# Latent attention's fp32 products written as three one-pass products of high and low parts

## The chip, the cores and the metric

The kernel runs on one core of a Trainium2 chip. The core has five engines, each with its own in-order queue: TensorE (PE, matrix products; its weight loads are listed as PEld), VectorE (DVE), ScalarE (ACT), GpSimd (POOL) and SyncE (SP, which issues nearly all transfers). The metric is the device time of one execution in microseconds (us): the median over runs. The profile is one further execution, with its own time.

## The reference

The reference is a decoder trunk with one layer of kind A and one of kind B, at 256 positions, width 2048. The change touches the latent attention of layer B alone:

```python
q = (rmsnorm(q_lat, g_q_lat) @ w_uq).reshape(B, S, MLA_HEADS, NOPE_DIM + ROPE_DIM)   # 12 heads, 128 + 64
q_nope = q[..., :NOPE_DIM]
q_rope = apply_rope(q[..., NOPE_DIM:], cos, sin)
# per block of 128 queries
qa = jnp.einsum('bqhn,rhn->bqhr', qn, w_uk)
s = (jnp.einsum('bqhr,bkr->bhqk', qa, c_kv) + jnp.einsum('bqhp,bkp->bhqk', qr, k_rope)) * scale
s = jnp.where(k_pos[None, :] <= q_pos[:, None], s, -jnp.inf)
p = jax.nn.softmax(s, axis=-1)
o_lat = jnp.einsum('bhqk,bkr->bqhr', p, c_kv)
return jnp.einsum('bqhr,rhv->bqhv', o_lat, w_uv)
```

All arrays are fp32. Beside it stand a four-head attention into 256 memory tokens, the output projection, a gated feed-forward network and, after both layers, a final norm.

## The kernel before

Activations lie feature-major: 128 features on the partitions, 256 positions along the free axis. Every large weight product is made of *parts*: a number is split into a high part (rounded by a copy into the type fp32r, which the TensorE multiplies in one pass) and a low part (the rest, also fp32r). Activations hold both parts side by side, high in columns 0 to 255, low in 256 to 511 (`xhl`, `qhl`, `chl`, `mainhl`). `chunk` loads a piece of a weight (`raw`), ACT copies it to `whi`, DVE subtracts to get `wlo`; `mm_fm` multiplies `whi` with all 512 columns (line 158) and `wlo` with the high 256 (line 162). `join` adds the two halves of the result (ACT copies one out of PSUM into `cr`, DVE adds). `wlo` tiles for stationary use begin 19 floats into their buffer.

The latent attention does not use parts. It runs after the projections: `values` makes the values of all heads by `gemm_tm` (lines 213 to 215) and evicts them as fp32 into `scratch`. Then a loop over six pairs of heads, `i` = 0 to 5, issues for each pair: `queries` (three 128-row blocks: two heads' plain queries and one block with both heads' rotary parts, into the fp32 tile `qn`), `keys` (two blocks into `kn`), `rotary` (one product of the rotary block with a permutation `swap`, line 857, then DVE and POOL form `qr`), `scores` per head (lines 947 to 949), `turn` (three transposes of the probabilities, line 970, copied by ACT into `pT`) and `attend` (lines 979 and 980). Scores of a pair come one iteration after its queries and keys, `turn` and `attend` one iteration later still. The memory attention (`mscores`, `mturn`, `mout`; lines 575, 599, 610) is spread over the same iterations. The last turns and attends run as hooks inside the output projection.

In `scores`, the first block of 128 queries sees 128 keys and the second 256, so each of the two products (plain and rotary) is made once with 128 columns and once with 256; between them a bf16 product with 128 columns adds the causal mask (line 948). All these products are fp32. In the hardware's records one fp32 matmul is two rows (two weight loads, two matmuls), one fp32r matmul is one row. `attend` is a 256-column and a 128-column product per head.

The program text gives priorities only. A scheduler that simulates the engines sets the order on each engine when the kernel is built; that order is then fixed, and each engine takes its instructions strictly in turn. PSUM has eight tiles, `cr` and `js` two buffers each, `raw`, `whi` and `wlo` four.

Of the kernel before, what the change touches and what calls it, by code (L numbers as in the profile page):

```python
# [8 lines left out]
F32 = mybir.dt.float32  # L9
# [60 lines left out]
class Kernel:  # L70
# [247 lines left out]
    def masks(self):  # L318
# [14 lines left out]
        self.identb = cp.tile([P, P], BF16, name="identb")  # L333
        nc.vector.tensor_copy(self.identb, self.ident)
        self.maskb = cp.tile([P, P], BF16, name="maskb")
        m = self.gp.tile([P, P], F32, name="mask")
# [257 lines left out]
    def memory_turn(self, p, pool, bufs=2):  # L594
        nc = self.nc
        acc = self.psum()
        for mb in range(2):
            for sb in range(2):
                nc.tensor.transpose(  # L599
                    acc[:, mb * S + sb * P : mb * S + (sb + 1) * P], p[:, sb, mb * P : (mb + 1) * P], self.ident  # L600
                )
        pT = self.tmp(pool, [P, 512], "pT", bufs)
        nc.scalar.activation(pT, acc, AF.Copy)
# [204 lines left out]
    def layer_b(self):  # L808
# [9 lines left out]
        with tc.tile_pool(name="lb", bufs=1) as lb:  # L818
            ctx = ExitStack()
            qhl = lb.tile([P, 4, 512], F32R, name="qhl")  # L820
            chl = lb.tile([P, 4, 512], F32R, name="chl")

            krz = lb.tile([P, 2, S], F32, name="krz")
            nc.gpsimd.memset(krz, 0.0)
            qm = lb.tile([P, MH, S], F32, name="qm1")
            lt = ctx.enter_context(tc.tile_pool(name="lt", bufs=1))

# [26 lines left out]

            def rotate(dst, a):
                acc = self.psum()
                mm(acc[:, :S], self.swap, a, start=True, stop=True)
                m = self.tmp(lb, [P, S], "rm", 1)
                nc.gpsimd.tensor_tensor(m, a, self.cosT, ALU.mult)
                tt(dst, acc[:, :S], self.sinT, ALU.mult)  # L860
                nc.gpsimd.tensor_tensor(dst, dst, m, ALU.add)
# [13 lines left out]
            def rotate_key():  # L875
# [17 lines left out]
            hl = self.ap.tile([P, NB, 512], F32R, tag="big", name=self.uid("mainhl"))  # L893
            scratch = self.ap.tile([P, NB * 512], F32, tag="xhl", name="scratch")
            v = scratch[:, : 2 * GW].rearrange("p (a c) -> p a c", a=2)
# [15 lines left out]
            scale = HD ** -0.5  # L911
            qn, qr, kn, pa, pm = {}, {}, {}, {}, {}

            def queries(pr):
                accs = [self.psum() for _ in range(3)]
                src = self.rows(wuq, pr * 2 * HD, 2 * HD)
                for c in range(0, 4, 2):
# [5 lines left out]
                    self.mm_fm(jobs, c > 0)  # L923
                qn[pr] = self.tmp(lp, [P, 3, S], "qn", 2)
                for j in (2, 0, 1):
                    self.join(accs[j], qn[pr][:, j, :])

            def keys(pr):
                kn[pr] = self.tmp(lp, [P, 2, S], "kn", 2)

                def ev(b, acc):
                    self.join(acc, kn[pr][:, b, :])

                self.gemm_fm(self.rows(wuk, pr * 256, 256), list(range(4)), 2, lambda k: chl[:, k, :], ev, nk=4)

            def rotary(pr):
                qr[pr] = self.tmp(lp, [P, S], "qr", 2)
                rotate(qr[pr], qn[pr][:, 2, :])

            def scores(h):  # L940
                pr, j = divmod(h, 2)
                sc = self.psum()
                for qb in range(2):
                    n = P * (qb + 1)
                    o = sc[:, qb * P : qb * P + n]
                    q = slice(qb * P, (qb + 1) * P)
                    mm(o, qn[pr][:, j, q], kn[pr][:, j, :n], start=True, stop=False)  # L947
                    mm(o[:, qb * P :], self.identb, self.maskb, start=False, stop=False)
                    mm(o, qr[pr][:, q], krz[:, j, :n], start=False, stop=True)  # L949
                mx = self.tmp(lp, [P, 2], "mx", 4)  # L950
# [15 lines left out]
            def turn(h):  # L966
                p = pa.pop(h)
                acc = self.psum()
                for i in range(3):
                    nc.tensor.transpose(acc[:, i * P : (i + 1) * P], p[:, i * P : (i + 1) * P], self.ident)  # L970
                pT = self.tmp(lp, [P, 512], "pT", 3)
                nc.scalar.activation(pT[:, : 3 * P], acc[:, : 3 * P], AF.Copy)
                pa[h] = pT

            def attend(h):
                pT = pa.pop(h)
                o = self.psum()
                cols = slice(h * P, (h + 1) * P)
                mm(o[:, :S], v[:, 0, cols], pT[:, :S], start=True, stop=False)  # L979
                mm(o[:, P:S], v[:, 1, cols], pT[:, S : S + P], start=False, stop=True)  # L980
                self.split(hl[:, h, :], o[:, :S])
# [4 lines left out]
            def mturn(h):  # L986
                pm[h] = self.memory_turn(pm[h], lp, 3)

# [135 lines left out]
```

## Time and profile before

| | |
|---|---|
| median of 3 runs | 2075.89 us (2075.86 to 2075.90) |
| profiled execution, its own time | 2076.27 us |
| its span | 2074.6 us |
| TensorE busy in the span | 99% |
| VectorE, ScalarE, GpSimd busy | 70%, 55%, 19% |
| TensorE clock granted | 0.998 |
| where the attention loop lies | about 1171 to 1252 us, its last two heads up to about 1270 us |

In a timeline row the columns are start (us from the span's start), duration from the first start to the last end (us), engine, line, operation, tiles written and read, shape, count and, in brackets, idle time of the engine before it with what ended it. A matmul's duration includes the time it takes to drain, which overlaps the next one; the pace of matmuls is read from the distance between starts. [...]

### The profile page before, as it was taken

The numbers are of one execution on the slowest core, as the hardware profiler recorded it, in microseconds if no ns is written. First come the engines' busy times: TensorE is split into PE (matmuls) and PEld (weight loads), VectorE is DVE, ScalarE is ACT, GpSimd is POOL, SyncE is SP. The second block draws the span as 40 slices with busy tenths as digits, with TensorE's granted clock in tenths as the row PEclk, the third lists the DMA queues.
The fourth block names the chain that finished last, engine by engine and source line by source line (L and its number), as shares of the span: only waits on it lengthen the run. The fifth ranks groups of instructions, "written<-read, shape, count | busy, mean of one in ns | idle before, by whom it ended". The sixth has DMA issues, their size and how long they took to land.

```text
span 2074.6 us, 31012 instructions
## 1 busy us (share of the span) xinstructions
PE 2064.0 (99%) x11614; PEld 1803.8 (87%) x11614; DVE 1460.5 (70%) x2150; ACT 1138.7 (55%) x1747; POOL 397.3 (19%) x387
## 2 busy tenths in 40 slices
PE   9999999999999999999999999999999999999998
PEld 8888888888888888888888888888888888888886
DVE  6655767777756877568798875777774677746875
ACT  7754654665535655455555664466653565535654
POOL 0100133322101222012254121421210222101220
PEclk9999999999999999999999999999999999999999
DMA  8575556666556666666565534566666666566664
GB/s 279 194 216 162 163 191 195 191 187 201 194 193 193 184 203 194 192 192 191 186 198 178 178 108 163 186 189 184 195 198 193 185 192 196 200 193 190 186 193 153
DMA packets 208092, 392.01 MB, mean 189 GB/s; under 512 B 14334, under 2 KB 23876, under 8 KB 207812
## 3 DMA queue, kind: packets, MB, share of 16 engines
q1 hardware_dynamic: 207364, 388.98, 60.1%
q8 instruction: 91, 1.49, 0.3%
q10 hardware_dynamic: 576, 1.05, 0.2%
q14 instruction: 61, 0.50, 0.1%
HBM read 387.88 MB, written 2.10 MB: 188 GB/s over the span
## 4 chain that ended last, share of the span: by engine, by line
PE 99%; ACT 0%; DVE 0%; issue 0%; ACTq 0%
PE ps L158 52%; PE ps L162 26%; PE ps L214 6%; PE ps L213 6%; PE ps L215 6%; PE ps L949 0%; PE ps L947 0%; PE ps L575 0%; PE ps L432 0%; PE ps L610 0%; PE ps L979 0%; PE ps L760 0%; PE ps L513 0%; PE ps L872 0%; PE ps L970 0%; PE ps L599 0%
## 5 line engine op out<-in xcount | busy, mean ns | idle before, releaser
L118 DVE TENSOR_TENSOR wlo<-raw,whi 128x1024 fp32r<-128x1024 f32 x660 | 842.8, 1287 | 453.2 <-ACT whi L117 338.6
L117 ACT ACTIVATE whi<-raw 128x1024 fp32r<-128x1024 f32 x660 | 695.6, 1058 | 677.3 <-PE ps L158 499.1
L158 PE MATMUL ps<-xhl,whi 128*128 128x512 f32 x3264 | 765.2, 390 | 0.0
L158 PEld LDWEIGHTS ps<-xhl,whi 128*128 128x128 f32 x3264 | 604.9, 188 | 121.2
L662 POOL TENSOR_TENSOR a<-js,rbc 128x256 f32<-128x256 f32 x176 | 230.7, 1323 | 1082.4 <-DVE js L264 986.7
L162 PEld LDWEIGHTS ps<-xhl,wlo 128*128 128x128 f32 x3264 | 388.9, 188 | 8.4
L162 PE MATMUL ps<-xhl,wlo 128*128 128x256 f32 x3264 | 392.2, 277 | 0.0
L158 PE MATMUL ps<-h,whi 128*128 128x512 f32 x704 | 164.8, 390 | 0.0
L665 ACT ACTIVATE c<-a,cT 128x256 f32<-128x256 f32 x176 | 105.2, 598 | 96.7 <-POOL a L662 95.2
L158 PEld LDWEIGHTS ps<-h,whi 128*128 128x128 f32 x704 | 130.4, 188 | 26.0
L214 PE MATMUL ps<-wlo,h 128*128 128x512 f32 x354 | 137.1, 388 | 0.0
L213 PE MATMUL ps<-whi,h 128*128 128x512 f32 x354 | 137.0, 388 | 0.0
L215 PE MATMUL ps<-whi,h 128*128 128x512 f32 x354 | 136.6, 388 | 0.0
L158 PE MATMUL ps<-mainhl,whi 128*128 128x512 f32 x512 | 120.1, 390 | 0.0
L158 PEld LDWEIGHTS ps<-mainhl,whi 128*128 128x128 f32 x512 | 94.7, 188 | 18.9
L667 DVE SCALAR_TENSOR_TENSOR c<-a,cT,c 128x254 f32<-128x254 f32 x176 | 101.0, 586 | 0.0
L666 DVE SCALAR_TENSOR_TENSOR c<-a,cT,c 128x255 f32<-128x255 f32 x176 | 91.7, 540 | 11.6 <-ACT c L665 11.4
L123 DVE SCALAR_TENSOR_TENSOR wlo<-raw,gT,whi 128x512 fp32r<-128x512 f32 x112 | 87.4, 822 | 16.9 <-ACT whi L122 15.3
L264 DVE TENSOR_TENSOR js<-ps,cr 128x256 f32<-128x256 f32 x209 | 82.3, 416 | 12.4 <-POOL a L662 12.4
L122 ACT ACTIVATE whi<-raw,gT 128x512 fp32r<-128x512 f32 x112 | 74.8, 722 | 29.3 <-PE ps L158 14.9
L262 ACT ACTIVATE cr<-ps 128x256 f32<-128x256 f32 x243 | 79.7, 374 | 16.2 <-PE ps L158 12.0
L162 PEld LDWEIGHTS ps<-h,wlo 128*128 128x128 f32 x704 | 83.9, 188 | 1.9
(259 smaller groups left out, 1852.5 us busy)
## 6 DMA issues: line engine op xcount, KB each, us to landing
raw<-in_w_ffn_up SPq DMA_DIRECT2D x352, 512.0 KB, 3.7
raw<-in_w_ffn_down SPq DMA_DIRECT2D x176, 512.0 KB, 3.6
raw<-in_w_out SPq DMA_DIRECT2D x64, 512.0 KB, 3.5
raw<-in_w_in_a SPq DMA_DIRECT2D x56, 512.0 KB, 4.3
raw<-in_w_mem_kv SPq DMA_DIRECT2D x31, 512.0 KB, 4.3
raw<-in_w_in_b SPq DMA_DIRECT2D x16, 512.0 KB, 3.5
raw<-in_w_kv_a SPq DMA_DIRECT2D x9, 512.0 KB, 4.5
raw<-in_w_uq SPq DMA_DIRECT2D x12, 384.0 KB, 3.4
```

The lines of the kernel that those rows point to most:

```text
L117: nc.scalar.activation(hi[:, :n], raw[:, :n], AF.Copy)
L118: nc.vector.tensor_tensor(lo[:, :n], raw[:, :n], hi[:, :n].bitcast(F32), ALU.subtract)
L123: nc.vector.scalar_tensor_tensor(lo[:, s], raw[:, s], gains[k], hi[:, s].bitcast(F32), ALU.mult, ALU.subtract)
L158: mm(acc[:, :], wh, x, start=first, stop=last)
L162: mm(acc[:, S:], wl, x[:, :S], start=False, stop=False)
L213: mm(acc, xh, wh, start=first, stop=False)
L214: mm(acc, xh, wl, start=False, stop=False)
L215: mm(acc, xl, wh, start=False, stop=last)
L662: nc.gpsimd.tensor_tensor(a, self.join(acc), rb, ALU.mult)
L665: nc.scalar.activation(c, a, AF.Identity, scale=w(2), bias=w(3))
L666: nc.vector.scalar_tensor_tensor(c[:, 1:], a[:, : S - 1], w(1), c[:, 1:], ALU.mult, ALU.add)
L667: nc.vector.scalar_tensor_tensor(c[:, 2:], a[:, : S - 2], w(0), c[:, 2:], ALU.mult, ALU.add)
```

## The change

`parts` splits a tile into a high and a low fp32r tile: a copy on ACT and a subtraction, on DVE unless POOL is named. `mm_parts` multiplies two split tiles as high by high, high by low and low by high, all added up in PSUM; low by low is left out. With them:

- the plain and rotary products of `scores` and the two products of `attend` become three fp32r products each;
- the rotary permutation becomes two fp32r products (`swapr`, an exact copy of `swap`, with the two parts of the rotary block);
- the operands are split: queries' low parts and keys' low parts on POOL; the rotary block (`rp`), rotated queries (`qr`), rotary keys (`krhl`), values and turned probabilities on DVE; all high parts on ACT;
- queries and keys pass through the two `js` buffers instead of being written by `join` straight to their tiles;
- buffers: `pT` goes from three to two (now inside `scratch`), the memory attention's copy `mpT` and `qr` have one each;
- in the loop, `rotary(i - 1)` is written ahead of `queries(i)`, and the last `rotary` behind the scores of the pair before.

```diff
+    def parts(self, hi, lo, x, engine=None):
+        self.nc.scalar.activation(hi, x, AF.Copy)
+        (engine or self.nc.vector).tensor_tensor(lo, x, hi.bitcast(F32), ALU.subtract)
+    def mm_parts(self, out, w, m, start, stop):
+        mm = self.nc.tensor.matmul
+        mm(out, w[0], m[0], start=start, stop=False)
+        mm(out, w[0], m[1], start=False, stop=False)
+        mm(out, w[1], m[0], start=False, stop=stop)
...
-            def rotate(dst, a):
+            def rotate(dst, a, parts):
                 acc = self.psum()
-                mm(acc[:, :S], self.swap, a, start=True, stop=True)
+                for i in range(2):
+                    mm(acc[:, :S], self.swapr, parts[:, i, :], start=i == 0, stop=i == 1)
...
+                for j in range(2):
+                    self.parts(krhl[:, j, 0, :], krhl[:, j, 1, :], krz[:, j, :])
...
-                    nc.scalar.activation(v[:, tb, c * 512 : (c + 1) * 512], acc, AF.Copy)
+                    cols = slice(c * 512, (c + 1) * 512)
+                    self.parts(v[:, 0, tb, cols], v[:, 1, tb, cols], acc)
...
                 for j in (2, 0, 1):
-                    self.join(accs[j], qn[pr][:, j, :])
+                    o = self.join(accs[j], ro[pr] if j == 2 else None)
+                    dst = rp[pr] if j == 2 else qn[pr][:, j]
+                    self.parts(dst[:, 0, :], dst[:, 1, :], o, None if j == 2 else nc.gpsimd)
...
-                    self.join(acc, kn[pr][:, b, :])
+                    self.parts(kn[pr][:, b, 0, :], kn[pr][:, b, 1, :], self.join(acc), nc.gpsimd)
...
-                qr[pr] = self.tmp(lp, [P, S], "qr", 2)
-                rotate(qr[pr], qn[pr][:, 2, :])
+                rq = self.tmp(lp, [P, S], "rq", 1)
+                rotate(rq, ro[pr], rp[pr])
+                qr[pr] = self.tmp(lp, [P, 512 + 64], "qr", 1, F32R)[:, 19 : 19 + 512].rearrange("p (i s) -> p i s", i=2)
+                self.parts(qr[pr][:, 0, :], qr[pr][:, 1, :], rq)
...
-                    mm(o, qn[pr][:, j, q], kn[pr][:, j, :n], start=True, stop=False)
+                    both_parts = lambda x, c: (x[:, 0, c], x[:, 1, c])
+                    self.mm_parts(o, both_parts(qn[pr][:, j], q), both_parts(kn[pr][:, j], slice(0, n)), True, False)
                     mm(o[:, qb * P :], self.identb, self.maskb, start=False, stop=False)
-                    mm(o, qr[pr][:, q], krz[:, j, :n], start=False, stop=True)
+                    self.mm_parts(o, both_parts(qr[pr], q), both_parts(krhl[:, j], slice(0, n)), False, True)
...
-                pT = self.tmp(lp, [P, 512], "pT", 3)
-                nc.scalar.activation(pT[:, : 3 * P], acc[:, : 3 * P], AF.Copy)
+                pT = pTs[:, h % 2]
+                self.parts(pT[:, 0, :], pT[:, 1, :], acc[:, : 3 * P])
...
-                mm(o[:, :S], v[:, 0, cols], pT[:, :S], start=True, stop=False)
-                mm(o[:, P:S], v[:, 1, cols], pT[:, S : S + P], start=False, stop=True)
+                for a, c, s in ((0, slice(0, S), slice(0, S)), (1, slice(P, S), slice(S, S + P))):
+                    self.mm_parts(o[:, c], (v[:, 0, a, cols], v[:, 1, a, cols]), (pT[:, 0, s], pT[:, 1, s]), a == 0, a == 1)
...
             for i in range(n):
-                queries(i)
                 if i >= 1:
                     rotary(i - 1)
+                queries(i)
...
-                if i == n - 1:
-                    rotary(i)
                 if i >= 1:
                     scores(2 * i - 2)
                     scores(2 * i - 1)
+                if i == n - 1:
+                    rotary(i)
```

The built order on TensorE is the same before and after outside the attention; inside it three places matter below.

The first is TensorE at the end of the first pair's queries. Before (the last three rows of `queries(0)`, then the first two of `queries(1)`):

```order
L158 MATMUL ps_11797<-qhl,whi_11821 128x512 x2
L158 MATMUL ps_11798<-qhl,whi_11821 128x512 x2
L158 MATMUL ps_11799<-qhl,whi_11821 128x512 x2
L158 MATMUL ps_11850<-qhl,whi_11854 128x512 x2
L158 MATMUL ps_11851<-qhl,whi_11854 128x512 x2
```

After (`rp` is the split rotary block, made from the PSUM tile of the third row here, `ps_11818`):

```order
L158 MATMUL ps_11816<-qhl,whi_11840 128x512 x2
L158 MATMUL ps_11817<-qhl,whi_11840 128x512 x2
L158 MATMUL ps_11818<-qhl,whi_11840 128x512 x2
L873 MATMUL ps_11880<-rp_11861,swapr 128x256
L158 MATMUL ps_11890<-qhl,whi_11894 128x512 x2
```

The first rotary product now stands directly behind the product whose result it needs.

The second is ScalarE in the same place, where the high part of `rp` is made. After (`cr` is the copy out of PSUM for `join`, `ro` the joined rotary block):

```order
L262 ACTIVATE cr_11862<-ps_11818 128x256
L262 ACTIVATE cr_11867<-ps_11816 128x256
L113 ACTIVATE whi_12070<-raw_12069 128x2x256
L113 ACTIVATE whi_12070<-raw_12069 128x2x128
L274 ACTIVATE rp_11861<-ro_11860 128x256
```

Between the copy out of PSUM and the high part of `rp` stand another copy and two pieces of a weight chunk.

The third is VectorE after the scores of the first head. Before (`mx` the negated maximum, `den` the sum, `p` the probabilities):

```order
L961 RECIPROCAL den_11949<-den_11949 128x2
L956 TENSOR_SCALAR mx_11966<-mx_11966 128x2
L582 TENSOR_SCALAR mx_11980<-mx_11980 128x2
L963 TENSOR_SCALAR p_11950<-p_11950,den_11949 128x128
L963 TENSOR_SCALAR p_11950<-p_11950,den_11949 128x256
L114 TENSOR_TENSOR wlo_12189<-raw_12187,whi_12188 128x2x256
```

After:

```order
L876 TENSOR_TENSOR rq_12055<-ps_12056,sinT 128x256
L985 TENSOR_SCALAR mx_12031<-mx_12031 128x2
L990 RECIPROCAL den_12006<-den_12006 128x2
L596 TENSOR_SCALAR mx_12045<-mx_12045 128x2
L114 TENSOR_TENSOR wlo_12309<-raw_12307,whi_12308 128x2x256
L992 TENSOR_SCALAR p_12007<-p_12007,den_12006 128x128
L992 TENSOR_SCALAR p_12007<-p_12007,den_12006 128x256
```

A piece of a weight's low part (`wlo`), which itself follows a ScalarE copy behind the first head's exponentials, now stands ahead of the scaling of the probabilities, and the rotary multiplication (`rq`) ahead of both.

More of the change, by code (lines that the diff above doesn't have):

```diff
@@ L334, in masks @@
         nc.vector.tensor_copy(self.identb, self.ident)
+        self.swapr = cp.tile([P, P], F32R, name="swapr")
+        nc.vector.tensor_copy(self.swapr, self.swap)
         self.maskb = cp.tile([P, P], BF16, name="maskb")
@@ L601, in memory_turn @@
                 )
-        pT = self.tmp(pool, [P, 512], "pT", bufs)
+        pT = self.tmp(pool, [P, 512], "mpT", bufs)
         nc.scalar.activation(pT, acc, AF.Copy)
@@ L821, in layer_b @@
             chl = lb.tile([P, 4, 512], F32R, name="chl")
-            krz = lb.tile([P, 2, S], F32, name="krz")
+            qm = lb.tile([P, MH, S], F32, name="qm1")
+            krhl = lb.tile([P, 2, 2, S], F32R, name="krhl")
+            lt = ctx.enter_context(tc.tile_pool(name="lt", bufs=1))
+            krz = lt.tile([P, 2, S], F32, name="krz")
             nc.gpsimd.memset(krz, 0.0)
-            qm = lb.tile([P, MH, S], F32, name="qm1")
-            lt = ctx.enter_context(tc.tile_pool(name="lt", bufs=1))
             both = lt.tile([P, 2, P], F32, name="both")
@@ L893, in layer_b @@
             hl = self.ap.tile([P, NB, 512], F32R, tag="big", name=self.uid("mainhl"))
-            scratch = self.ap.tile([P, NB * 512], F32, tag="xhl", name="scratch")
-            v = scratch[:, : 2 * GW].rearrange("p (a c) -> p a c", a=2)
+            scratch = self.ap.tile([P, NB * 512], F32R, tag="xhl", name="scratch")
+            v = scratch[:, 19 : 19 + 4 * GW].rearrange("p (i a c) -> p i a c", i=2, a=2)
+            pTs = scratch[:, 4 * GW + 64 : 4 * GW + 64 + 12 * P].rearrange("p (n i s) -> p n i s", n=2, i=2)
             wuv = t["w_uv"][0].rearrange("r h v -> r (h v)")
@@ L911, in layer_b @@
             scale = HD ** -0.5
-            qn, qr, kn, pa, pm = {}, {}, {}, {}, {}
+            qn, qr, kn, ro, rp, pa, pm = {}, {}, {}, {}, {}, {}, {}
             def queries(pr):
@@ L986, in mturn @@
             def mturn(h):
-                pm[h] = self.memory_turn(pm[h], lp, 3)
+                pm[h] = self.memory_turn(pm[h], lp, 1)
             def mout(h):
```

6 lines of the change are left out of this document (4 added, 2 removed).

## The prediction

> **What bounds the kernel now.** I read the page first, then the list of what TensorE waits for, then the timelines of the attention, because the change touches only that stage. From the page:
>
> ```profile
> span 2074.6 us, 31012 instructions
> PE 2064.0 (99%) x11614; PEld 1803.8 (87%) x11614; DVE 1460.5 (70%) x2150; ACT 1138.7 (55%) x1747; POOL 397.3 (19%) x387
> PE 99%; ACT 0%; DVE 0%; issue 0%; ACTq 0%
> ```
>
> TensorE is busy throughout, and the chain that ended last is TensorE alone. So the time moves by what TensorE's own instructions take and by any new wait of TensorE; work added to other engines costs nothing until TensorE waits for it. In the whole attention TensorE waits once:
>
> ```profile
> PE ps L979 <- ACT pT L972: 0.3, 1, 0.3
> ```
>
> So what counts is the pace of single matmuls. From TensorE's timeline, starts in the first column:
>
> ```profile
> 1185.07 0.39 PE L947 MATMUL ps<-kn,qn 128*128 128x128 f32 x2
> 1185.29 0.22 PE L948 MATMUL ps<-maskb,identb 128*128 128x128 bf16 x1
> 1185.35 0.44 PE L947 MATMUL ps<-kn,qn 128*128 128x128 f32 x2
> 1185.62 0.22 PE L948 MATMUL ps<-maskb,identb 128*128 128x128 bf16 x1
> ...
> 1200.54 0.59 PE L979 MATMUL ps<-pT,scratch 128*128 128x256 f32 x2
> 1200.97 0.38 PE L980 MATMUL ps<-pT,scratch 128*128 128x128 f32 x2
> ```
>
> An fp32 product is two rows. Two rows with 128 columns take 0.22 us (1185.07 to 1185.29), two with 256 columns 0.43 (1200.54 to 1200.97): 0.11 and 0.216 us a row, as two streams of the columns each would. The mask, one pass of 128 columns, takes 0.06 (1185.29 to 1185.35). But the pair after the mask takes 0.27 instead of 0.22 (1185.35 to 1185.62). Nothing in it is longer; its first weights were not there yet. [...]
>
> One-pass fp32r rows exist with 256 columns:
>
> ```profile
> 1174.97 1.54 PE L162 MATMUL ps<-qhl,wlo 128*128 128x256 f32 x12
> 1176.34 2.91 PE L158 MATMUL ps<-qhl,whi 128*128 128x512 f32 x12
> ```
>
> Twelve in 1.37 us, 0.115 each. No fp32r row with 128 columns exists before.
>
> **The change, part by part: TensorE.** The rows it replaces, counted:
>
> ```profile
> L857 PE MATMUL ps<-qn,swap x12: 377/378/382, 1181.8 to 1241.5; 128*128 128x256 f32 x12
> L947 PE MATMUL ps<-kn,qn x48: 272/354/382, 1185.1 to 1249.2; 128*128 128x128 f32 x24, 128*128 128x256 f32 x24
> L949 PE MATMUL ps<-krz,qr x48: 272/354/435, 1186.6 to 1249.7; 128*128 128x128 f32 x24, 128*128 128x256 f32 x24
> L979 PE MATMUL ps<-pT,scratch x24: 377/379/483, 1200.5 to 1269.4; 128*128 128x256 f32 x24
> L980 PE MATMUL ps<-pT,scratch x24: 272/274/275, 1201.0 to 1269.7; 128*128 128x128 f32 x24
> ```
>
> That is 72 rows with 128 columns (24 + 24 + 24) at 0.11, 7.9 us, and 84 with 256 (12 + 24 + 24 + 24) at 0.216, 18.1 us: 26.1 us in all. After, each product is three rows: 12 heads with two score products and one of values, 108 rows with 128 columns and 108 with 256, and 12 rotary rows with 256. The 120 wide ones cost 120 x 0.115 = 13.8 us. The narrow ones are unknown. Their lower bound is the mask's 0.06, one pass of the same columns; the upper one the 0.216 of a wide fp32 row. I take 0.11, the load pace, because three different weights, or the same one loaded again, precede them, and the loads look alike:
>
> ```profile
> L948 PEld LDWEIGHTS <-identb x24: 97/98/100, 1185.2 to 1249.2; 128*128 128x128 bf16 x24
> L947 PEld LDWEIGHTS ps<-kn,qn x48: 188/192/192, 1184.8 to 1249.0; 128*128 128x128 f32 x48
> L162 PEld LDWEIGHTS ps<-qhl,wlo x72: 187/188/192, 1174.7 to 1235.3; 128*128 128x128 f32 x72
> ```
>
> The load of fp32r (L162) lasts 188 ns, that of fp32 (L947) 192, that of the bf16 mask 98. So 108 x 0.11 = 11.9 us, less 0.05 for each of the 12 narrow rows that stand ahead of a mask, whose load is short: 11.3. Sum 25.1 us against 26.1: **TensorE's own work shrinks by 1.0 us**, although passes fall from four to three: a narrow product goes from 0.22 to 0.33 us, a wide one from 0.43 to 0.35, and the permutation, two rows for two, from 0.43 to 0.23. The 24 waits behind masks stay. With the bounds, this term lies between -6.4 (0.06) and +11.0 us (0.216).
>
> [...]
>
> **The other engines.** Per pair of heads the change adds six copies on ACT (three queries' blocks, two keys' blocks, the rotated block), four subtractions on DVE (`rp`, `qr`, two of 384 columns out of PSUM) and four on POOL. A steady window and the rows that price them:
>
> ```profile
> 1200.00:1215.00 15.00, 15.00 (x92) 13.23 (x91) 10.94 (x33) 9.49 (x30) 2.37 (x2) 1.00 0.32 98
> L262 ACT ACTIVATE cr<-ps 128x256 f32<-128x256 f32 x30 | 10.5, 385 | 12.1 <-PE ps L158 12.0
> L264 DVE TENSOR_TENSOR qn<-ps,cr 128x256 f32<-128x256 f32 x18 | 7.0, 414 | 0.9 <-ACT cr L262 0.9
> L859 POOL TENSOR_TENSOR rm<-qn,cosT 128x256 f32<-128x256 f32 x6 | 8.8, 1470 | 15.6 <-DVE qn L264 15.2
> ```
>
> The first is a window of 15 us, about one pair; busy us of PE, PEld, DVE, ACT, POOL in that order. ACT goes from 9.5 to 9.5 + 6 x 0.385 = 11.8 us, DVE from 10.9 to 10.9 + 2 x 0.414 + 2 x about 0.55 (an estimate between 256 columns and twice that) = 12.9, POOL from 2.4 to at most 2.4 + 4 x 1.47 = 8.3. None fills the 15 us, so none becomes the bound. What they add is latency, and keys, queries and turned probabilities are used some 6 us of TensorE work or more after they are made, in the next iteration. There I cost them at nothing; the cover is that work, and every us by which a split is later than it is lost in full. The six new subtractions for the values (about 0.7 us each, as 512 columns of weights below) and two for the rotary key fall into this stretch of DVE:
>
> ```profile
> 1165.74 2.35 DVE L118 TENSOR_TENSOR wlo<-raw,whi 128x1024 fp32r<-128x1024 f32 x2
> ...
> 1172.20 1.03 DVE L114 TENSOR_TENSOR wlo<-raw,whi 128x512 fp32r<-128x512 f32 x2 [1.74 <-ACT whi L113]
> ```
>
> DVE idles there, since weights are made ahead of need; I cost these at nothing too. Without that lead, each would be 0.7 us of waiting.
>
> Two places in the order have no cover. **First pair's rotation.** TensorE takes the first rotary row directly behind `queries(0)`; behind it, in turn, stands all of `queries(1)`. In the trace before:
>
> ```profile
> 1177.93 0.66 ACT L262 ACTIVATE cr<-ps 128x256 f32<-128x256 f32 x2 [1.70 <-PE ps L158]
> 1178.47 0.94 ACT L113 ACTIVATE whi<-raw 128x512 fp32r<-128x512 f32 x2
> ...
> 1178.35 0.76 DVE L264 TENSOR_TENSOR qn<-ps,cr 128x256 f32<-128x256 f32 x2 [0.86 <-ACT cr L262]
> ```
>
> The last of the six closing rows of `queries(0)` starts about 1177.5 (twelve rows of 0.23 from 1176.34, the first six of them this pair's), so TensorE is free at 1177.7. ACT's copies run from 1177.93, the two pieces of a weight chunk to 1179.41, and only then comes the high part of `rp`, 0.385: 1179.8. TensorE waits **2.1 us**, where before it went on at once. The least it can wait, were the weight pieces not in the way, is the drain, copy, addition and copy: about 1.4.
>
> **First head's probabilities.** The transpose of the first head stands behind its scores, the second head's scores (0.9 us), a rotary row and the rest of `queries(2)` (16 rows, 2.75 us): 3.8 us after the first head's scores. Before:
>
> ```profile
> 1187.31 0.87 PE L949 MATMUL ps<-krz,qr 128*128 128x256 f32 x4
> ...
> 1188.92 1.28 ACT L958 ACT_TABLE_LOAD   x1 [2.41 <-DVE mx L956]
> ...
> 1188.00 0.62 DVE L955 TENSOR_REDUCE mx<-ps 128x1 f32<-128x128 f32 x2 [0.67 <-PE ps L949]
> 1191.16 0.17 DVE L961 RECIPROCAL den<-den 128x2 f32<-128x2 f32 x1 [0.75 <-ACT p L958]
> 1191.37 0.54 DVE L963 TENSOR_SCALAR p<-p,den 128x128 f32<-128x128 f32 x2
> ...
> L113 ACT ACTIVATE whi<-raw 128x512 fp32r<-128x512 f32 x10 | 6.3, 630 | 0.6 <-PE ps L158 0.6
> L114 DVE TENSOR_TENSOR wlo<-raw,whi 128x512 fp32r<-128x512 f32 x11 | 7.9, 717 | 2.4 <-ACT whi L113 2.1
> ```
>
> From the first maximum to the reciprocal is 3.2 us (a table load of ACT is in it), and the maximum starts 0.2 after the scores, whose last two rows begin at 1187.31 and take 0.49 with the wait behind the mask. Now a piece of a weight copy (ACT, 0.63) and its low part (DVE, 0.72) stand between, then 0.3 of scaling: 0.2 + 3.2 + 1.3 + 0.3 = 5.0 us against 3.8: **1.2 us** of waiting, 0 if the pieces are quicker, 2 if they are later. The one wait before, behind the turns of the last heads but two, I leave as it is: its chain gets a copy and a subtraction, and its cover the new narrow rows.
>
> **Sum.** -1.0 + 2.1 + 1.2 = +2.3 us: the profile's 2076.27 becomes 2078.6, and against the runs' median of 2075.89, 0.4 lower than that execution, **2078.2 us**, a change of 0.11%. A measurement of this kernel can tell about 0.2%, some 4.2 us, from no change; between 2071.7 and 2080.0 counts as none.
>
> **Rivals.**
> (a) *The two waits do not come*, since what the order puts ahead is ready sooner than I reckon, or the time comes back. Then the 1.0 us of TensorE alone is left: 2074.9. For it speaks that the order before left one wait in the attention. Against it: the product directly behind its own source cannot be covered. Chance 0.13.
> (b) *The splits are late in every pair.* Place: the rotated queries, whose chain (DVE, POOL, ACT, DVE) is four engines long and starts at the head of the iteration, with DVE at 86% and POOL's queue shared with the low parts of queries and keys. Price: 1.2 us in each of the four later iterations, 4.8 on top, 2083.0; it decides from about 0.5 us each, 2080.2. Against it: some 8 us of TensorE work (queries and keys) lie between the rotation and its use, and the chain is drain 0.3, DVE 0.41, POOL up to 1.47, ACT 0.39, DVE 0.41, together 3.0, before other work in their queues. Chance 0.18, slower.
> (c) *A narrow fp32r row costs more than its load*, up to a wide fp32 row's 0.216: 108 x 0.1 = 11 us on top, about 2089. No row speaks for it; none excludes it. Chance 0.06, slower.
> (d) *The new weights load as fast as the mask's*, so narrow rows run at 0.06: 5.4 us less, 2072.8. Against it are the 188 ns of fp32r loads beside 98. Chance 0.06; it would be faster by over 0.2% only without the waits too.
> [...]
>
> **Numbers.** The forecast itself, with waits of 2 to 5 us in all, has 0.57, its own range 2076.9 to 2080.0 (2074.9 and 2 to 5 more), with a little of it above. For 8 in 10 I leave out (c), (d) and the upper half of (b): 2074.4 to 2082.4. Faster by over 0.2%: 0.03, from (d) without waits. Slower: (b), (c) and the forecast's upper end, 0.25. Within: 0.72.
>
> **What would show it.** Right: the fp32r rows of 128 columns in the scores start 0.11 us apart, those of 256 0.115; the list of TensorE's waits has line 873 waiting about 2 us for `rp` and line 999 about 1 us for `p`, each once; DVE near 13 and ACT near 12 us of 15 in a steady window; nothing outside the attention changed. Wrong: narrow rows at 0.06 or 0.2; waits repeated in each pair on `qr`, `kn` or turned probabilities; or a changed pace of lines 158 and 162 throughout, since the new `swapr` tile moves most buffers by 512 bytes, which I cost at nothing.

## The result and the profile after

| | before | after |
|---|---|---|
| median of 19 runs each | 2076.30 us | 2079.92 us |
| lowest and highest run | 2075.86, 2077.14 | 2079.30, 2082.40 |
| profiled execution, its own time | 2076.27 us | 2079.34 us |
| ratio, 95% interval | | 1.0018 (1.0011 to 1.0025) |

The change makes the kernel 3.6 us slower (2079.92 - 2076.30), 0.18%. That lies inside the range and, by the middle of the interval, just within what counts as no change, but 1.7 us above the forecast of 2078.2; 0.4 of these are the base, which was 2075.89 over three runs and is 2076.30 over nineteen. Three executions beside the experiments, two of the kernel before and one of the rotation in its second order, took 2970 to 11269 us and are left out of the ratios and counts. The page after:

```profile
span 2077.6 us, 31255 instructions
PE 2065.0 (99%) x11686; PEld 1806.6 (87%) x11686; DVE 1478.0 (71%) x2183; ACT 1149.5 (55%) x1785; POOL 412.5 (20%) x411
```

and the list of what TensorE waits for:

```profile
PE ps L873 <- POOL kn L275: 2.0, 1, 2.0
PE ps L527 <- DVE ones L324: 1.1, 1, 1.1
PE ps L999 <- DVE p L992: 0.9, 1, 0.9
PE ps L370 <- DMA graw<-in_g_mem: 0.2, 1, 0.2
```

Two waits are new in the attention, at lines 873 and 999, once each; the 0.3 at the turned probabilities of the last heads is gone. The rows of lines 527 and 370 lie in the first 4 us of the program. How much the attention itself lost is read from two rows that stand ahead of it and behind it in both kernels. TensorE's timeline before, the first row of `queries(0)` and a block of the output projection:

```profile
1173.60 1.08 PE L158 MATMUL ps<-qhl,whi 128*128 128x512 f32 x4
...
1290.96 2.22 PE L162 MATMUL ps<-mainhl,wlo 128*128 128x256 f32 x18
```

and after:

```profile
1173.89 0.85 PE L158 MATMUL ps<-qhl,whi 128*128 128x512 f32 x3
...
1294.02 2.22 PE L162 MATMUL ps<-mainhl,wlo 128*128 128x256 f32 x18
```

The first pair differs by 0.29 us, the second by 3.06: the attention costs 2.8 us more in these two executions. The 0.3 ahead of it is there from the first microseconds on and is not the change's: in the traces of the experiments below, whose program has nothing new ahead of the attention but the same small tile or less, that number lies between -0.85 and +0.79. Between the two profiled executions lie 3.07 us, these 2.8 and the 0.3; between the medians lie 3.6. Most of the rest goes with the granted clock. Of the 19 executions of the changed kernel the nine quickest (up to 2079.69, middle 2079.48) have a mean granted clock of 0.999, the ten slowest (from 2079.92, middle 2080.7) one of 0.998; the last section has what the traces show of that. The profiled execution is one of the nine.

**TensorE's own rows.** The scores of the first head, after (starts in the first column):

```profile
1187.39 0.22 PE L280 MATMUL ps<-kn,qn 128*128 128x128 f32 x1
1187.45 0.27 PE L281 MATMUL ps<-kn,qn 128*128 128x128 f32 x1
1187.56 0.28 PE L282 MATMUL ps<-kn,qn 128*128 128x128 f32 x1
1187.68 0.23 PE L977 MATMUL ps<-maskb,identb 128*128 128x128 bf16 x1
...
1191.10 0.33 PE L280 MATMUL ps<-kn,qn 128*128 128x256 f32 x1
1191.27 0.28 PE L281 MATMUL ps<-kn,qn 128*128 128x256 f32 x1
1191.39 0.28 PE L282 MATMUL ps<-kn,qn 128*128 128x256 f32 x1
```

Rows of 128 columns stand 0.11 us apart, rows of 256 columns 0.12. (Next to a row of another width starts are shifted by some 0.05, as 1187.39 to 1187.45 and 1191.10 to 1191.27 show, 0.06 and 0.17; therefore the sums here go from the end of one row to the end of the next.) Over the whole attention the mean is 0.112 for a narrow row behind a narrow one and 0.117 for a wide one behind a wide one, and the mask's row takes 0.072 behind an fp32r row where it took 0.056 behind fp32. Their loads, in the view by line:

```profile
L281 PEld LDWEIGHTS ps<-kn,qn x24: 187/192/192, 1187.4 to 1253.4; 128*128 128x128 f32 x24
```

are as long as before (188/192/192 ns at line 947). Replaced rows with their masks took 28.77 us from end to end (the wait at line 979 taken off), the new ones 28.32 (the wait at line 873 taken off): **0.45 us less**, not 1.0.

**The rotation.** TensorE and, below it, ACT and DVE around the first rotation:

```profile
1176.64 1.55 PE L158 MATMUL ps<-qhl,whi 128*128 128x512 f32 x6
1180.17 0.36 PE L873 MATMUL ps<-rp,swapr 128*128 128x256 f32 x1 [1.98 <-POOL kn L275]
```

```profile
1176.78 1.06 ACT L117 ACTIVATE whi<-raw 128x1024 fp32r<-128x1024 f32 x1 [0.62 <-DMA raw<-in_w_uk]
1177.75 0.40 ACT L274 ACTIVATE kn<-js 128x256 fp32r<-128x256 f32 x1
1178.28 0.66 ACT L262 ACTIVATE cr<-ps 128x256 f32<-128x256 f32 x2
1178.83 0.94 ACT L113 ACTIVATE whi<-raw 128x512 fp32r<-128x512 f32 x2
1179.65 0.42 ACT L274 ACTIVATE rp<-ro 128x256 fp32r<-128x256 f32 x1
```

```profile
1177.88 1.23 DVE L118 TENSOR_TENSOR wlo<-raw,whi 128x1024 fp32r<-128x1024 f32 x1 [0.90 <-ACT whi L117]
1179.02 0.42 DVE L264 TENSOR_TENSOR ro<-ps,cr 128x256 f32<-128x256 f32 x1
```

The high part of `rp` ends at 1180.07 and the rotation follows; the name in brackets after it is that of the shared helper line, not of `kn`. ACT runs two copies, two pieces of a weight and then `rp`, as the order had it. Ahead of them there is something the prediction had not seen: ACT, in its turn, waits 0.62 us for the transfer of a chunk of `w_uk`. In this execution that costs next to nothing: ACT copies out of PSUM from 1178.28 on, 0.1 us behind the end of TensorE's last row (1176.64 + 1.55). DVE is held by the same chunk: its subtraction stands ahead of the addition that makes `ro`, which is done at 1179.44. Without the two weight pieces on ACT, `rp` would thus have begun only 0.2 us earlier.

**The first head's probabilities.** DVE, then TensorE:

```profile
1192.18 0.62 DVE L984 TENSOR_REDUCE mx<-ps 128x1 f32<-128x128 f32 x2 [1.02 <-PE ps L282]
...
1195.33 0.17 DVE L990 RECIPROCAL den<-den 128x2 f32<-128x2 f32 x1 [0.58 <-ACT p L987]
...
1195.85 0.69 DVE L114 TENSOR_TENSOR wlo<-raw,whi 128x512 fp32r<-128x512 f32 x1 [0.27 <-ACT whi L113]
1196.46 0.54 DVE L992 TENSOR_SCALAR p<-p,den 128x128 f32<-128x128 f32 x2
```

```profile
1194.92 1.09 PE L158 MATMUL ps<-qhl,whi 128*128 128x512 f32 x4
1196.88 0.30 PE L999 MATMUL ps<-ident,p 128*128 128x128 f32 x1 [0.87 <-DVE p L992]
```

From the maximum to the reciprocal 3.15 us, the weight's piece and its way through ACT 1.1, then the scaling: the chain as it was reckoned.

The steady window (PE, PEld, DVE, ACT, POOL busy) after:

```profile
1200.00:1215.00 15.00, 15.00 (x107) 13.74 (x106) 13.96 (x37) 12.16 (x39) 5.24 (x8) 1.00 0.31 92
```

DVE comes close to full (13.96 of 15 us), ACT less so (12.16), and TensorE waits for neither.

So the 2.8 us (2.77) are, from end to end: +2.22 at line 873, +1.06 at line 999, -0.45 own rows, -0.52 for the wait that went, and +0.46 spread over the other rows of the stage, about half of it the queries' (1 to 2 ns on each).

### The profile page after: what moved, and what is told of

Its sections match the earlier page's. It is cut to its first block, busy times and chain, and to the rows that moved or that the text cites. A ratio compares the mean times of both kernels' runs of the same rounds, so it can differ in the third digit from the quotient of the medians.

```text
span 2077.6 us, 31255 instructions
## 1 busy us (share of the span) xinstructions
PE 2065.0 (99%) x11686; PEld 1806.6 (87%) x11686; DVE 1478.0 (71%) x2183; ACT 1149.5 (55%) x1785; POOL 412.5 (20%) x411
## 4 chain that ended last, share of the span: by engine, by line
PE 97%; DVE 2%; DMA 0%; issue 0%; ACT 0%; POOL 0%; ACTq 0%; DVEq 0%
PE ps L158 51%; PE ps L162 25%; PE ps L213 6%; PE ps L214 6%; PE ps L215 6%; PE ps L280 0%; PE ps L281 0%; PE ps L446 0%; PE ps L282 0%; PE ps L589 0%; PE ps L624 0%; PE ps L774 0%; DVE wlo L123 0%; DMA raw<-in_w_uk 0%; PE ps L999 0%
## 5 line engine op out<-in xcount | busy, mean ns | idle before, releaser
L264 DVE TENSOR_TENSOR js<-ps,cr 128x256 f32<-128x256 f32 x233 | 92.1, 417 | 12.3 <-POOL a L676 12.3
L162 PE MATMUL ps<-h,wlo 128*128 128x256 f32 x704 | 84.3, 277 | 0.0
```

The costliest lines, as they stand in the source:

```text
L162: mm(acc[:, S:], wl, x[:, :S], start=False, stop=False)
L264: self.nc.vector.tensor_tensor(o, acc[:, :S], cr, ALU.add)
```

## Experiments

### What a narrow row costs

```diff
-        mm(out, w[0], m[0], start=start, stop=False)
-        mm(out, w[0], m[1], start=False, stop=False)
-        mm(out, w[1], m[0], start=False, stop=stop)
+        step = 64 if out.shape[-1] == P else out.shape[-1]
+        for a, b, first, last in ((0, 0, start, False), (0, 1, False, False), (1, 0, False, stop)):
+            for c in range(0, out.shape[-1], step):
+                self.nc.tensor.matmul(out[:, c : c + step], w[a], m[b][:, c : c + step], start=first and c == 0, stop=last and c > 0 or last and step > 64)
```

> The changed kernel, with each of the 108 narrow rows cut into two of 64 columns with the same weights; the same sums are made. Theory (a narrow row costs its weight load, 0.11 us, whatever its columns): 108 more rows at 0.11, +11.9 us, 2091.8, and the rows with 64 columns start 0.11 apart. Rival (fp32r streams 128 columns at half the pace, so the columns cost the 0.11): two rows of 64 take what one of 128 took, 2079.9, 0.055 apart. Rival (both share it): in between, about 2086.

Measured: 2091.60 us, 11.7 more than the changed kernel. The first product, six rows of 64 columns up to the mask:

```profile
1189.24 0.75 PE L282 MATMUL ps<-kn,qn 128*128 128x64 f32 x6
1189.83 0.23 PE L977 MATMUL ps<-maskb,identb 128*128 128x128 bf16 x1
```

Six rows of 64 columns take 0.59 us, three of 128 took 0.29 above, both by starts, the first of them next to a row of another width. From end to end over the whole attention, a row of 64 columns behind another takes 0.112 us (179 of them), and so does one of 128 in the changed kernel (71). Between these two widths the columns do not matter. What is left is a price of the row, and its load of weights (187 to 203 ns here; in the changed kernel the loads of lines 281 and 282 begin 0.11 us apart, at 1187.40 and 1187.51, and so overlap) fits it; the bf16 mask, whose load takes 96 ns there, goes at 0.07. That it is the load and nothing else that is fixed in an fp32r row, no run separates. (The total agrees partly by luck: this execution has a longer wait at line 873 and the half clock described in the last section, and lacks the wait at line 999.)

### The two waits, one at a time

First the wait at line 999:

```diff
-                if i >= 2:
+                if i >= 3:
                     turn(2 * i - 4)
                 if i >= 1:
                     keys(i)
+                if i == 2:
+                    turn(0)
```

> The changed kernel with one move: in the third iteration the transpose of the first head's probabilities is written behind the keys of that pair instead of ahead of them. Theory (the wait of line 999 is the probabilities being late, once): that wait of 0.9 us goes, all else stays, 2079.0 against 2079.9; the wait of 2.0 us at line 873 stays. Rival (whatever is late there moves the wait to the next product): 2079.9, and another wait of about 1 us on p or on a turned tile shows.

Measured: 2080.78 us (2078.96 to 2082.79); not faster. The wait at line 999 is gone, but the first values' products now stand close behind the transposes:

```profile
1203.07 0.47 PE L280 MATMUL ps<-scratch 128*128 128x256 f32 x2 [0.36 <-DVE js L264]
1203.78 0.39 PE L281 MATMUL ps<-scratch 128*128 128x256 f32 x1 [0.24 <-DVE scratch L275]
```

which is 1.1 us more from end to end: the rival was right for this move alone. (The profiled execution, 2078.96, is the quickest and the only one of the eleven with a mean clock of 0.999; the other ten, with 0.998, begin at 2079.80.) And line 873's wait is 2.40 us in this execution. ACT shows why it is longer than the 1.98 above:

```profile
1176.64 1.06 ACT L117 ACTIVATE whi<-raw 128x1024 fp32r<-128x1024 f32 x1 [1.24 <-DMA raw<-in_w_uk]
```

In three executions with the same order there, the wait for this transfer was 0.62, 1.24 and 1.30 us, and the weight's copy began 0.14, 0.75 and 1.10 us after the first of the closing rows of `queries(0)`; TensorE then waited 1.98, 2.40 and 2.75 us. The uncovered rotation hands the landing time of a weight on to TensorE, once that is late enough.

Then the wait at line 873, by the order of rotary that the kernel had before (with a second buffer for `ro` and `rp`):

```diff
+                queries(i)
                 if i >= 1:
                     rotary(i - 1)
-                queries(i)
```

> The changed kernel with rotary written behind queries again, as before the change, in every iteration; ro and rp get two buffers for it. Theory: the wait of 2.0 us at line 873 goes, since all of the second pair's queries now lies between the first rotary block and its rotation. But the built order now has the first head's transpose directly behind the second head's scores and one rotary row, 1.0 + 0.1 us of cover instead of 3.8, against a chain of 5.0: the wait at line 999 grows from 0.9 to about 3.9. Sum: 2079.9 - 2.1 - 0.9 + 3.9 = 2080.8. Rival (the order of rotary alone is what costs the time): 2077.8.

Measured: 2084.36 us, 3.6 above the expectation though the mechanism is the expected one. The wait at line 873 is gone, that at line 999 has grown:

```profile
1198.89 0.45 PE L999 MATMUL ps<-ident,p 128*128 128x128 f32 x1 [5.29 <-DVE p L992]
1198.99 2.91 PE L158 MATMUL ps<-chl,whi 128*128 128x512 f32 x6
1201.70 1.54 PE L162 MATMUL ps<-chl,wlo 128*128 128x256 f32 x8
```

5.3 instead of 3.9 us. And then the six rows of line 158 take 2.71 us, not 1.45 as behind line 999 in the changed kernel: after the wait TensorE ran at about half its pace. The window says the same (the number after POOL is the granted clock):

```profile
1199.00:1202.00 3.00, 3.00 (x9) 2.42 (x10) 1.99 (x8) 1.24 (x6) 0.60 (x1) 0.50 0.02 5
```

That costs some 1.7 us, and a new wait of 1.0 us on a turned tile at the end of the attention covers the rest of the 3.6 (1.4 are the longer wait).

Both moves together:

> Both moves together: rotary behind queries, and the first head's transpose behind the third pair's keys. Theory: no wait at line 873; the first head's transpose has the second head's scores, a rotary row and the keys before it, 3.9 us against a chain of 5.0, so 0 to 1.1 us at line 999: 2076.9 to 2078.0. If no wait is left and the time is still above 2078.5, the narrow products or something spread over the pairs cost more than the rows show.

Measured: 2086.59 us, 8.6 above the upper end of the expectation. Line 999 waits four times, 4.9 us in all, and the clock stays at one half for longer (10.2 us, from 1199.0 to 1209.2):

```profile
PE ps L999 <- DVE p L992: 4.9, 4, 2.9
PE ps L280 <- ACT scratch L274: 1.0, 1, 1.0
```

Writing rotary behind queries is thus no repair: the built order then has all of the third pair's queries ahead of the first scores' last rows, and what is left (16 rows of keys, 2.8 us) does not cover the probabilities.

### Cover for the rotation that moves nothing else

```diff
+            queries(0)
             keys(0)
             for i in range(n):
                 if i >= 1:
                     rotary(i - 1)
-                queries(i)
+                    queries(i)
```

> The changed kernel with the first pair's queries written ahead of its keys, so that the keys (16 rows, 2.8 us) lie between the first rotary block and its rotation; nothing else moves, and no buffer is added. Theory (line 873's wait of 2.0 to 2.8 us is the uncovered way through ACT, with a weight copy ahead that itself waits for its transfer, and its spread is what spreads the runs): the wait goes, 2079.9 - 2.1 - 0.4 of its mean excess = 2077.4, with 0.9 left at line 999, and the runs lie within 1 us of each other instead of 3. Rival (the products in parts cost more all along): 2079 or more.

Measured: 2077.79 us (2076.82 to 2079.07), ratio to the kernel before 1.0008 (0.9999 to 1.0016). The waits:

```profile
PE ps L999 <- DVE p L992: 1.5, 1, 1.5
PE ps L873 <- issue: 0.4, 1, 0.4
```

Line 873 keeps 0.4 of its 2.0 us and the kernel gains 2.1, although line 999 waits 0.6 longer in this trace. With the wait at line 873 the lower clock goes too: one execution of eleven has a mean of 0.998. The second half of the expectation failed: the runs still lie 2.25 us apart, so neither that wait nor the clock is all of the spread.

With the later first transpose as well:

> The changed kernel, all products in parts, with both moves: the first pair's queries ahead of its keys, and the first head's transpose behind the third pair's keys. Theory (the change's own work on TensorE is about 0.3 us less, and what it costs is the two waits): no wait over 0.7 us, and the time of the kernel before within 0.6: 2075.7 to 2076.9. Rival (the parts cost TensorE more all along, or the splits come late in later pairs): 2077.5 or more without one large wait.

Measured: 2076.95 us (2076.39 to 2078.37), ratio 1.0004 (0.9995 to 1.0014); the longest wait in the attention is

```profile
PE ps L280 <- DVE js L264: 0.4, 1, 0.4
```

Two moves that change no product take back 3.0 of the 3.6 us. So the change cost the waits and what came with them, and its products in parts are worth nothing measurable by themselves.

### Parts of the change alone

The rotation alone, in the kernel before:

```diff
-                mm(acc[:, :S], self.swap, a, start=True, stop=True)
+                for i in range(2):
+                    mm(acc[:, :S], self.swapr, parts[:, i, :], start=i == 0, stop=i == 1)
```

> The kernel before with the rotation alone in parts (swapr, two fp32r rows of 256 columns for two fp32 ones), the order of the text as before; its block is split by a copy on ACT and a subtraction on DVE. Theory: 6 x 0.2 = 1.2 us less of TensorE and no wait, since the next pair's queries lie between: 2075.1 against 2076.3. Rival (the new tile of 512 bytes, which shifts most buffers, or the start of the program costs 0.3 us): 2075.4. Rival (the split delays the first head's probabilities as in the changed kernel): 2076 to 2077 with a wait on p.

Measured: 2079.42 us (2078.84 to 2081.44); the expectation was 4.3 too low, and the rival that names the wait was 2.4 too low still. The six rotations do take 1.2 us less, but

```profile
PE ps L977 <- DVE p L970: 3.0, 1, 3.0
```

The transposes of the first head (line 977 here) wait for its probabilities. A copy and a subtraction more in the way of `qr` were enough for the scheduler to draw most of the third pair's queries ahead of the first scores, which before had stood between scores and transpose. (Here too the quicker executions, up to 2079.41, have a mean clock of 0.999 and the six slower ones 0.998.) With rotary ahead of queries and `queries(0)` ahead of `keys(0)`, the built order has them behind the scores again:

> The rotation alone in parts, with rotary ahead of queries and the first pair's queries ahead of its keys; the built order has all of the third pair's queries between the first scores and the first transpose, as in the kernel before. Theory (the 3 us of the earlier rotary-only kernel were the probabilities' chain, uncovered because the queries had moved ahead of the scores): no wait at the transposes, 1.2 us less than before, 2075.0. Rival (splitting the rotary block itself costs the time): 2078 or more.

Measured: 2075.48 us, ratio 0.9997 (0.9988 to 1.0007), 3.9 less with the same products. The waits on `p` are gone; the one that the kernel before had too is left:

```profile
PE ps L986 <- ACT pT L979: 0.5, 1, 0.5
```

Now parts for the wide products only, narrow ones in fp32 (the diff's core; the fp32 operands are kept beside the parts):

```diff
+                mm(o, qf[pr][:, j, q], kf[pr][:, j, q], start=True, stop=False)
+                mm(o, self.identb, self.maskb, start=False, stop=False)
+                mm(o, rf[pr][:, q], krz[:, j, q], start=False, stop=True)
+                o = sc[:, P : P + S]
+                self.mm_parts(o, two(qn[pr][:, j]), two(kn[pr][:, j]), True, False)
+                mm(o[:, P:], self.identb, self.maskb, start=False, stop=False)
+                self.mm_parts(o, two(qr[pr]), two(krhl[:, j]), False, True)
...
+                self.mm_parts(o[:, :S], (v[:, 0, cols], v[:, 1, cols]), (pT[:, 0, :], pT[:, 1, :]), True, False)
+                mm(o[:, P:S], v1[:, cols], pf, start=False, stop=True)
```

> Parts only where the columns are 256: the second query block's scores, the first key block's values and the rotation; all products with 128 columns stay fp32 as before. Order and transposes as in the kernel with both moves. Theory (a wide product falls from 0.43 to 0.35 us, a rotation from 0.43 to 0.23, narrow ones gain nothing): 36 x 0.083 = 3.0 and 6 x 0.2 = 1.2 us less than before, plus 12 masks behind fp32r rows at 0.015, plus 0 to 1.1 us of waiting: 2072.3 to 2073.4 against 2076.3. Rival (the narrow rows are not what ate the gain): 2076 or more. Rival (the extra copies make the splits late): waits on qn, kn or qr tiles in several pairs, over 2075.

Measured: 2077.94 us, 4.5 above the upper end of the expectation, in the order that failed above (rotary behind queries, the first transpose later): 2.6 us of waiting for `p`, then half the clock.

```profile
1202.00:1204.00 2.00, 2.00 (x12) 1.94 (x11) 0.59 (x2) 0.85 (x3) 1.29 (x2) 0.50 0.60 151
```

The same products in the repaired order:

> Parts only where the columns are 256 (second query block's scores, first key block's values, rotation), narrow products fp32; rotary ahead of queries and the first pair's queries ahead of its keys; transposes as in the changed kernel. In the built order all of the third pair's queries now lies between the first two heads' scores and the first transpose, as in the kernel before. Theory from the rows (wide products 0.43 to 0.35, rotation 0.43 to 0.23): 36 x 0.083 + 1.2 - 0.2 = 4.0 us less, no wait: 2072.3. By what the earlier kernel with these parts shows once its waits are taken off (1.7 us less): 2074.6. Rival (the parts' copies come late somewhere): 2076 or more, with a wait on a part in several pairs.

Measured: **2073.88 us** (2073.50 to 2074.77), ratio 0.9989 (0.9980 to 0.9998). One wait is left in the attention, where the expectation from the rows (2072.3) had none:

```profile
PE ps L1010 <- DVE p L1003: 1.1, 1, 1.1
```

The changed products with their masks take 25.1 us from end to end against 28.8, 3.7 less, close to the 4.0 from the rows. With the later first transpose:

> The kernel with parts for 256 columns only, queries(0) ahead of keys(0), and now also the first head's transpose behind the third pair's keys. Theory: its last wait of 1.1 us at the first transpose goes, but the turned probabilities of the first two heads are used sooner after their transposes, which cost 0.4 and 0.2 us in the changed kernel with that move: 2073.9 - 1.1 + 0.6 = 2073.4. Rival: the wait moves whole to the values' products, 2073.9.

Measured: **2073.53 us** (2072.53 to 2074.68), ratio 0.9987 (0.9979 to 0.9996). It beats both kernels, by 2.8 us the one before and by 6.4 us the changed one; at 0.13% the first is less than the 0.2% that count as a change here, but its interval leaves no change out. From the run before it, it cannot be told apart.

## Why the prediction was right, and where it was wrong

- **Narrow rows at 0.11**: right (0.112), and the rows of 64 columns, at 0.112 too, show that it is a price of the row and not of its columns. That it is the pace of weight loads, as reckoned, no run shows; the loads of these rows last 187 to 192 ns and begin as far apart as the rows do, 0.11 us.
- **TensorE's own work, -1.0 us**: mis-sized; it was -0.45. Wide rows took 0.117 instead of 0.115 (120 of them: 0.3), narrow ones 0.112 instead of 0.110 (108: 0.2), and the mask 0.016 more behind an fp32r row (24: 0.4), some 0.9 in all. Of that 0.3 does not show in the measured sum; it lies, as far as the rows show, at the edges next to rows of other kinds. No run shows the 0.05 less of a narrow row ahead of a mask: from end to end it took 0.112 there too; behind a mask the first narrow row took 0.115 where in fp32 it took 0.165, and over 12 masks the two come out even, at 0.6 each.
- **First rotation, 2.1 us**: right in place, cause and size (2.0 in the profile). What failed is the spread: the term had the weight pieces that ACT copies but not the transfer for which ACT waits ahead of them, and with it 2.4 and 2.75 us occur. Nor did it have DVE's share of that chunk ahead of `ro`: the 1.4 us that it gives as the least without the weight pieces on ACT would have been 1.8 here.
- **First head's probabilities, 1.2 us**: right; 0.9, since 4.0 us of TensorE work stood there, not 3.8.
- **The wait at the tail, left as it is**: it went, 0.5 us for the change.
- **Splits, values and rotary key at nothing**: right. In the steady window DVE has 13.96 us (12.9 reckoned), ACT 12.16 (11.8), POOL 5.24 (at most 8.3), and no wait comes from them. Rival (b) falls.
- **The shift of buffers at nothing**: right; between the feed-forward network of layer A and the attention the two executions keep the same distance of 0.3 us.
- **Rivals (a), (c), (d)**: fall; the waits came, and narrow rows, at 0.112 in turn, cost neither 0.2 nor 0.06.

The sum of the terms, +2.3, became +2.8 in the profile. Between the medians it is 3.6: the profiled execution of the changed kernel is one of its quicker ones (2079.34 against 2079.92), and its runs lie 3.1 us apart where those of before lie 1.3 apart. The step that failed is thus the sum's own-work term by 0.55 us, and, as an argument, that each wait was given one size and no price beyond its length. The sum has no term for the granted clock, and the ten executions in which its mean is 0.998 lie some 1.2 us above the nine others, as much as the half clock cost in the trace with 64-column rows. The wait at line 873 goes with it: without the wait at line 999 it stays in ten executions of eleven, without the one at line 873 it is in one. No trace shows such an execution of the changed kernel, so this is read from the mean clocks alone. That 2079.92 lies inside the range is therefore in part luck. What spreads the runs beyond that is open.

## What to carry to other kernels

Count a short product by its rows as well as its columns: here three one-pass rows of 128 columns cost 0.34 us (0.112 each) where the fp32 product cost 0.22, three of 256 columns 0.35 (0.117 each) against 0.43, and the kernels that split the wide ones and the rotation and left the narrow ones took 2.4 and 2.8 us less than the one before. A product placed directly behind the one whose result it needs pays the whole way through the other engines, with whatever stands in their queues and the transfers that those wait for (1.98, 2.40 and 2.75 us at line 873); and such a wait can cost more by a lower clock behind it (1.2 us behind the 2.75). Where a scheduler sets the order, look after every edit at the first turn of a software pipeline: a copy more in one chain moved a whole block of matmuls away from the chain that it had covered, and that cost more than the edit was worth (a wait of 3.0 us in the rotation alone, for 1.2 us less of its own work).

## What the hardware showed beside it

Around some waits TensorE was granted half its clock, which cost 1.2 to 1.7 us on top of the wait in the two traces where it is worked out here. With the 64-column rows, behind a wait of 2.75 us:

```profile
1180.55 0.55 PE L873 MATMUL ps<-rp,swapr 128*128 128x256 f32 x1 [2.75 <-POOL kn L275]
1180.90 2.76 PE L158 MATMUL ps<-qhl,whi 128*128 128x512 f32 x6
```

Six rows in 2.56 us, where the same six took 1.36 in the changed kernel. Windows of 1 us show where the granted clock changed:

```profile
1180.00:1181.00 1.00, 0.45 (x2) 0.48 (x3) 1.00 (x2) 1.00 (x4) 0.94 (x2) 0.64 0.62 149
1183.00:1184.00 1.00, 1.00 (x6) 0.87 (x5) 0.03 (x1) 0.72 (x2) 0.45 (x1) 0.66 0.46 81
```

Between these two it is 0.50, and outside them 1.00. It was thus half from 1180.28 (0.28 of full and 0.72 of half make 0.64) to 1183.68, for 3.4 us, and fell 2.5 us into the wait. Read in the same way, it was half for 3.4 us in the first kernel with mixed products too, from 1.0 us behind waits of 0.6, 2.0 and 0.5 on; for 6.8 us around the wait of 5.3; and for 10.2 us around the four waits of the kernel with rotary behind queries and the later transpose.

The mean clock of an execution shows such a stretch, as half of 3.4 us is 0.0008 of 2079 us:

| kernel | longest waits of TensorE in the attention, in its trace | executions with a mean clock of 0.998 or less |
|---|---|---|
| before (its executions beside the experiments) | 0.3 | 15 of 82 |
| changed | 2.0, 0.9 | 10 of 19 |
| first transpose later | 2.4 | 10 of 11 |
| `queries(0)` ahead of `keys(0)` | 1.5 | 1 of 11 |
| the two above together | 0.4 | 1 of 11 |
| rotation alone, first order | 3.0 | 6 of 11 |
| 64-column rows | 2.75 | 4 of 4 |

The figure is rounded, and the clock is half at the end of the program too: in the trace of before from 2068.3 us to the end of the span (6.3 us), in that of the changed kernel from 2073.1 (4.5 us), TensorE's last rows having ended at 2066.1 and 2069.2. This half clock alone puts the mean at 0.9985 and 0.9989. So a single 0.998 proves nothing: the 15 of the kernel before are no slower than its others (2076.25 against 2076.34). In the changed kernel and in the rotation alone the executions with 0.998 are the slowest ones without exception.

In the rotary-only kernel a wait of 3.0 us was followed by the full clock in the profiled execution:

```profile
1196.00:1198.00 2.00, 1.61 (x8) 1.40 (x9) 2.00 (x5) 2.00 (x10) 0.75 (x2) 1.00 0.00 0
```

So the length of a wait alone does not decide: the clock fell in the wait of 2.75 us and stayed full behind that of 3.0. The lengths read above, 3.4, 6.8 and 10.2 us, are one, two and three times 3.4; what sets them, and when the clock falls, no run shows.
